# An encoder trunk whose engine order is planned: new prices in the planner, a later request for the norm rows, another packing

## The chip, the cores and the metric

The kernel runs on one core of a Trainium2 chip. The metric is the device time of one execution in microseconds; the median of three executions stands for it. One more execution was profiled, and everything that is read below from a trace comes from that one.

## The reference

Two layers work on x of 512 positions by 1024 features, all in float32. One layer computes

```
h = RMSNorm(x);  z = h @ w_in                 # 1024 x 4352: q,k,v of branch A, q,k,v of branch B, gates ga, gb
A = windowed attention (8 heads, 2 kv heads, RoPE, sink, window 128)
B = 2-D neighbourhood attention (8 heads, 8x16 window on an 8x64 grid, relative bias)
x = x + (sigmoid(ga) * (A @ w_proj_a) + sigmoid(gb) * (B @ w_proj_b)) @ w_out
x = x + (silu(h' @ w_gate) * (h' @ w_up)) @ w_down     # h' = RMSNorm(x), hidden width 2816
```

In both attention branches q and k are normalised per head before the scores, and the softmax runs over at most 384 (A) or 256 (B) keys of a query.

## The kernel before

x is held transposed, as eight tiles `xT[k]` of 128 features by 512 positions. Every large product is made of float32r products: each operand is split into a high part (a cast on ScalarE) and a low part (the subtraction on VectorE, or an accumulating DMA), and a block of 128 by 128 by 512 takes three matmuls: high by high, high by low, low by high. This is a *unit* of the main stream (`UNIT` in the code). `token_matmul` and `pair_matmul` yield after each unit.

A layer's main stream is `layer(l)`: q of branch A (32 units, `token_matmul`), k and v of branch A (16 units, `pair_matmul` with `kv_evac`), q and k of branch B, v of branch B, again q and k of branch B (32 units each), the gates (128 units), the two output projections of the branches (64), `w_out` (64), the first hidden block of the feed-forward part (16 for gate, 16 for up), and then five larger hidden blocks. For these a seven-product scheme of 2 by 2 quadrants is used: `m_step` does one of the seven products (24 matmuls of 256 columns) in the order 1, 5, 6, 2, 7, 3, 4. It needs a split of a combination of weights (class `Quad`) and a split of a combination of x's blocks (`chain_x`, which fills `xs[m]`). Behind product 1 a ScalarE copy (`seed`) puts its sum into a second PSUM bank, and product 6 adds to that bank.

Beside the main stream run *chains*, generators for the norm, the head norms, RoPE, each head of attention, the splits of x's blocks. A chain yields a `Need`: which tiles must be ready for which engine, which PSUM banks must be free. `Norm.chain` sums the squares on TensorE, computes the inverse root (`rsqrt`: some fourteen small VectorE operations, each on the result of the one before) and then turns the factor into rows with four transposes, which makes `nrm.rows`.

The order of each engine's instructions is fixed before the kernel runs, in a first pass without a chip: each call of an engine (class `Engine`) advances a clock of that engine by a price (`cost`), and writes down when the result is ready. A reader on another engine, or on the same one, sees it ready later by a hop (`HOPS`). A chain goes on when its `Need` is met at the main stream's clock: for TensorE the tiles must be ready `MARGIN` (0.3) ahead; for the others the engine's clock may lead TensorE's by at most a backlog (`BACKLOG` 1.0 us, `XLOG` 6.0 us). Where the main stream yields a name, as `f"rows{nrm.i}"`, `force` issues chains, with ever more slack, until that name is done. The second pass issues the same order, and every engine works its queue strictly in that order.

The first pass also notes from when to when each buffer is used. `Layout.pack` places the buffers in two arenas of fixed size: it tries five orders of placing, takes the first that fits, and then `spread` moves buffers so that one that takes the place of another comes long after it. `spread` returns a histogram of the time between the two, the shortest (negative) bin first.

Line 305 in all rows is the one line through which all instructions are issued, so the rows are told apart by tile: `mm` and `at` are PSUM banks (main products; attention, transposes and some quadrants), `arena` is any buffer, `sm` and `hf` are small tiles of factors, `rstd` the norm factor, `negm` the negative maximum of a score row, `gb` a column of gains.

Of the kernel before, what the change touches and what calls it, by code (L numbers as in the profile page):

```python
# [25 lines left out]
KD = D // P  # L26
FFN = 2816
QUADS = (FFN - 256) // 512
ARENAS = {F32: 20480, F32R: 32128}
# [4 lines left out]
XLOG = 6.0  # L34
# [61 lines left out]
class Layout:  # L96
# [40 lines left out]
    def pack(self):  # L137


        starts = [0] * len(self.sizes)  # L140
        self.slack = {}
        for kind in ARENAS:
            live = [i for i, k in enumerate(self.kinds) if k == kind and self.uses[i] is not None]
            u = np.array([self.uses[i] for i in live])
            size = np.array([self.sizes[i] for i in live])
            span = u[:, 1] - u[:, 0]
            orders = [
                np.lexsort((-span, -size)),
                np.argsort(-span * size, kind="stable"),
                np.argsort(-span, kind="stable"),  # L150
                np.lexsort((-span * size, -size > -1000)),
                np.lexsort((u[:, 0], -size)),
            ]
            at = next((f for o in orders if (f := self.packed(u, size, o, ARENAS[kind])) is not None), None)
            if at is None:
                raise RuntimeError(f"no room in the arena for {kind}")
            self.slack[kind] = self.spread(u, size, at, ARENAS[kind])
            for i, x in zip(live, at):
                starts[i] = int(x)
        self.starts = starts  # L160
        self.dry, self.count = False, 0
# [48 lines left out]
def trunk(ctx: ExitStack, tc: tile.TileContext, a: dict, out: bass.AP, lay: Layout):  # L210
# [20 lines left out]
    def buf(shape, dtype=F32):  # L231

        n = int(np.prod(shape))
        x = lay.place(n, dtype)
        t = arenas[dtype][:, x : x + n]
        if len(shape) == 2:
            t = t.rearrange("p (a b) -> p a b", b=shape[1])
        elif len(shape) == 3:
            t = t.rearrange("p (a b c) -> p a b c", b=shape[1], c=shape[2])
        return t  # L240
# [7 lines left out]
    def mm_bank():  # L248
        return pm.tile([P, S], F32, tag="mm", name=nm("mm"))
# [9 lines left out]

    clock = {"pe": 0.0, "dve": 0.0, "act": 0.0, "pool": 0.0, "dma": 0.0}  # L260
    ready = {}
    HOPS = {("pe", "dve"): 0.2, ("pe", "act"): 0.2, ("dve", "pe"): 0.26, ("act", "pe"): 0.3, ("dve", "dve"): 0.06}

    def at_(tensor, key):

        t, by = ready.get(tensor, (0.0, key))
        return t + HOPS.get((by, key), 0.0 if by == key else 0.15)


    def cost(eng, name, o, aps):  # L270
        n = max(x.free_size() for x in aps) / 1000.0
        in_psum = any(x.space == PS for x in aps[1:])
        if eng == "pe":
            cols = aps[2].free_size()
            if name == "transpose":
                return 0.1
            if aps[1].dtype == F32:
                return max(4 * cols, 256) / 2400.0 + 0.002
            return 0.12 if cols == 256 else (cols if cols >= 256 else 4 * cols) / 2255.0
        if eng == "act":  # L280
            return n * 0.833 + (0.06 if in_psum else 0.1) + 0.093 * sum(x.free_size() == 1 for x in aps[2:])
        if eng == "dve":
            fast = name in ("tensor_copy", "tensor_scalar") and not in_psum
            per = 0.52 if fast else 6.4 if name == "reciprocal" else 1.04
            return n * per + (0.13 if name == "scalar_tensor_tensor" and not in_psum else 0.075)
        return n * 2.2 + 0.1

    steps = [0]
# [143 lines left out]
    def tick(dt):  # L432
        pos[0] += dt
        while due and due[0][0] <= pos[0]:
            due.pop(0)[2]()
# [126 lines left out]
    def w_take():  # L562

        i = used[0]
        used[0] += 1
        w_load(i)
        w_low(i)
        return [(highs[i][:, k], lows[i][:, k]) for k in range(plan[i][0])]
# [108 lines left out]
    def mm(ps, l_, r_, start, stop):  # L677
        T.matmul(ps, l_, r_, start=start, stop=stop, skip_group_check=True)
# [58 lines left out]
    def gain(norm, k):  # L737
        c = 16 * (norm % 2) + 8 * (norm // 2) + k
        return vecT[:, c : c + 1]
# [117 lines left out]
    def pair_matmul(parts, xh, xl, evac):  # L857

        ps = [mm_bank(), mm_bank()]
        for k0 in range(0, parts, 4):  # L860
            n = min(4, parts - k0)
            wk = w_take()
            for j in range(2):
                c = slice(P * j, P * j + P)
                for k in range(n):
                    kk = k0 + k
                    hi, lo = wk[k]
                    mm(ps[j], hi[:, c], xh[kk], kk == 0, False)
                    mm(ps[j], hi[:, c], xl[kk], False, False)
                    mm(ps[j], lo[:, c], xh[kk], False, kk == parts - 1)  # L870
                    tick(UNIT)
                    if kk == parts - 1:
                        evac(j, ps[j])
                    yield UNIT
# [314 lines left out]
    def layer(l):  # L1189
        nrm = norms[2 * l]  # L1190
# [173 lines left out]

        yield from token_matmul(nrm, copy_to(qraw), (lambda *x: start(nrm, *x)) if l == 0 else None)
        done.add(f"q{l}")
        yield f"rows{nrm.i}"

        def kv_evac(j, ps):
            t = act()  # L1370
# [3 lines left out]
                V.tensor_tensor(by_columns(t), held(ps), held(nrm.rows), ALU.mult)  # L1374
            kv.append(t)

        yield from pair_matmul(KD, nrm.xh, nrm.xl, kv_evac)
        done.add(f"kv{l}")
        yield from token_matmul(nrm, copy_to(qk[0]))
        done.add(f"qk{l}0")  # L1380
# [58 lines left out]
        nrm = norms[2 * l + 1] = Norm(2 * l + 1)  # L1439
# [34 lines left out]
        def chain_x():  # L1474
            yield Need(keys=[f"rows{nrm.i}"])
            xn = [buf([4, S]) for _ in range(2)]
            (b11, b12), (b21, b22) = ((t[:, :, :256], t[:, :, 256:]) for t in xn)

            def normal(h):
                for i in range(4):  # L1480
                    yield Need(backlog=XLOG)
                    V.scalar_tensor_tensor(
                        xn[h][:, i], xT[4 * h + i], gain(nrm.i, 4 * h + i), nrm.rows, ALU.mult, ALU.mult
                    )

            def high(m, src):
                yield Need("act", [src], backlog=XLOG)
                h = buf([4, 256], F32R)
                A.copy(h, src)
                xs[m] = src, h  # L1490

            def low(m):
                src, h = xs[m]
                yield Need("dve", [h], backlog=XLOG)
                lo = buf([4, 256], F32R)
                V.tensor_tensor(lo, src, h.bitcast(F32), ALU.subtract)
                xs[m] = h, lo
                done.add(f"x{l}{m}")

            n1, n2 = buf([4, 256]), buf([4, 256])  # L1500
            yield from normal(0)
            yield from high(1, b11)
            V.tensor_tensor(n1, b11, b12, ALU.subtract)
            yield from low(1)
            yield from high(5, n1)
            yield from normal(1)
            V.scalar_tensor_tensor(n2, n1, -1.0, b22, ALU.mult, ALU.subtract)
            yield from high(6, n2)
            yield from low(5)
            yield from low(6)  # L1510
            yield from high(2, b21)
            yield from low(2)
            V.tensor_tensor(b12, b22, b12, ALU.subtract)
            yield from high(7, b12)
            yield from low(7)
            yield from high(3, b22)
            yield from low(3)
            V.scalar_tensor_tensor(n1, n2, -1.0, b21, ALU.mult, ALU.subtract)
            yield from high(4, n1)
            yield from low(4)  # L1520
# [4 lines left out]
        u = []  # L1525
# [122 lines left out]
        for i, step in enumerate(steps_[:-KD]):  # L1648
            if step[0] == "m":
                _, q, w, m = step  # L1650
# [4 lines left out]
            else:  # L1655
                _, f0, n, c = step
# [5 lines left out]
                o = mm_bank()  # L1662
# [4 lines left out]
        _, f0, n, _ = steps_[-1]  # L1667
# [12 lines left out]
    def main():  # L1680
        norms[0] = Norm(0)
        for l in range(DEPTH):
            yield from layer(l)
# [30 lines left out]
```

## Time and profile before

| what | us |
|---|---|
| median of three runs | 1396.6 |
| lowest and highest run | 1396.34 and 1397.06 |
| profiled execution, its own time | 1397.06 |
| its span in the trace | 1395.3 |
| TensorE busy in the span | 1374.3 |
| VectorE, ScalarE, GpSimd busy | 916.6, 699.5, 317.5 |

The span is the stretch from the first to the last instruction of the program; the profiled execution's own time is 1.8 us longer. A row of a timeline gives the start, the time to the end of the last of its instructions, and in brackets the idle time of that engine before it with the engine and tile that ended it. The attention part of the two layers lies at about 36 to 256 us and 720 to 939 us; the feed-forward quadrants begin at 379.6 and 1062.5 us.

### The profile page before, as it was taken

How to read it: one execution, taken by the hardware profiler on the slowest of the kernel's cores; microseconds unless marked ns; L12 is line 12 of the kernel's file. 1: busy time of each engine (PE TensorE's matmuls, PEld its weight loads, DVE VectorE, ACT ScalarE, POOL GpSimd, SP SyncE). 2: the span in 40 equal slices, each digit the busy share in tenths (PEclk: the TensorE clock that was granted, in tenths of full speed). 3: DMA queues.
4: the chain of work that ended last, by engine and by line, in shares of the span. 5: the costliest groups of instructions: out<-in, count | busy, mean ns of one | idle time of the engine just before them, and what ended most of it. 6: DMA issues, size and time to landing. Idle time of an engine off the chain costs nothing.

```text
span 1395.3 us, 20880 instructions
## 1 busy us (share of the span) xinstructions
PE 1374.3 (98%) x8042; PEld 1210.4 (87%) x8042; DVE 916.6 (66%) x1718; ACT 699.5 (50%) x1155; POOL 317.5 (23%) x326
## 2 busy tenths in 40 slices
PE   7999999999999999999999999999999999999998
PEld 5788888888899999999987888888888999999996
DVE  5876888455877566575648768773568747575653
ACT  6477667444644343343545776664356334333441
POOL 4443222310121020101353422223012110111110
PEclk9999999999999999999999999999999999999999
DMA  8888888974676475735799878889558583754645
GB/s 210 170 156 144 153 148 151 179 172 152 114 173 146 112 180 122 181 78 120 151 190 191 141 139 153 154 146 214 139 136 144 140 202 87 169 121 121 143 86 119
DMA packets 197331, 207.45 MB, mean 149 GB/s; under 512 B 25568, under 2 KB 167056, under 8 KB 197232
## 3 DMA queue, kind: packets, MB, share of 16 engines
q0 software_dynamic: 134976, 141.54, 54.7%
q1 hardware_dynamic: 61904, 64.04, 16.0%
q8 instruction: 63, 1.03, 0.3%
q10 hardware_dynamic: 352, 0.54, 0.1%
q14 instruction: 36, 0.29, 0.1%
HBM read 193.51 MB, written 2.10 MB: 140 GB/s over the span
## 4 chain that ended last, share of the span: by engine, by line
PE 82%; DVE 10%; DMA 3%; ACT 2%; issue 2%; POOL 0%; SPq 0%; DVEq 0%; ACTq 0%; POOLq 0%
PE mm L305 64%; PE at L305 18%; DVE arena L305 7%; DVE sm L305 3%; ACT arena L305 2%; DMA arena<-in_rel_bias_b 1%; DMA arena<-in_w_in 1%; DMA arena<-arena 1%; DMA cst<-in_consts 0%; DVE hf L305 0%; SPq L305 0%; POOL posi L305 0%; ACT L305 0%; POOL vec L305 0%; ACT mm L305 0%
## 5 line engine op out<-in xcount | busy, mean ns | idle before, releaser
L305 PE MATMUL mm<-arena 128*128 128x512 f32 (+1 forms) x5568 | 1114.3, 356 | 4.6 <-ACT arena L305 1.9
L305 PEld LDWEIGHTS mm<-arena 128*128 128x128 f32 x5568 | 905.0, 190 | 139.2 <-DVE arena L305 4.2
L305 ACT CAST arena<-arena 128x1024 fp32r<-128x1024 f32 (+2 forms) x278 | 235.5, 869 | 210.3 <-DVE arena L305 204.0
L305 DVE TENSOR_TENSOR arena<-arena,arena 128x1024 fp32r<-128x1024 f32 (+2 forms) x268 | 262.4, 994 | 60.7 <-ACT arena L305 60.1
L305 ACT ACTIVATE arena<-arena 128x1024 fp32r<-128x1024 f32 (+3 forms) x252 | 206.3, 842 | 155.3 <-DMA arena<-in_w_down 80.2
L305 PE MATMUL at<-arena 128*128 128x256 f32 (+1 forms) x1952 | 279.7, 288 | 1.3 <-DVE arena L305 1.3
L305 PEld LDWEIGHTS at<-arena 128*128 128x128 f32 x1952 | 258.6, 191 | 15.0 <-DVE arena L305 1.6
L305 DVE TENSOR_TENSOR arena<-arena,mm 128x512 f32<-128x512 f32 x144 | 98.8, 686 | 232.0 <-PE mm L305 232.0
L305 POOL DMA_DIRECT2D arena<-in_w_in x163 | 162.3, 1408 | 324.1 <-ACT arena L305 315.6
L305 POOL DMA_DIRECT2D arena<-in_w_down x96 | 98.1, 1229 | 500.9 <-ACT arena L305 389.2
L305 DVE TENSOR_TENSOR arena<-arena 128x1024 f32<-128x1024 f32 (+4 forms) x196 | 158.4, 823 | 2.4
L305 DVE TENSOR_TENSOR arena<-at,arena 128x512 fp32r<-128x512 f32 (+4 forms) x158 | 103.9, 659 | 26.1 <-ACT arena L305 21.0
L305 ACT CAST arena<-at 128x512 fp32r<-128x512 f32 (+2 forms) x116 | 64.1, 554 | 75.9 <-PE at L305 74.5
L305 PE MATMUL at<-cst,arena 128*128 128x128 f32 x472 | 74.9, 277 | 5.0 <-DVE arena L305 3.8
L305 ACT ACTIVATE arena<-arena,negm 128x256 f32<-128x256 f32 (+1 forms) x128 | 68.3, 534 | 18.0 <-DVE negm L305 16.4
L305 DVE TENSOR_TENSOR arena<-mm,arena 128x512 f32<-128x512 f32 x72 | 49.2, 686 | 39.2 <-PE mm L305 39.1
L305 PEld LDWEIGHTS at<-cst,arena 128*128 128x128 f32 x472 | 57.6, 141 | 19.2 <-DVE arena L305 4.5
L305 ACT COPY arena<-at 128x512 f32<-128x512 f32 (+1 forms) x68 | 39.5, 581 | 66.2 <-PE at L305 65.8
L305 DVE CUSTOM_DVE_ANT_0 arena<-at,cst,nsnk 128x256 f32<-128x256 f32 (+1 forms) x64 | 34.3, 547 | 29.9 <-PE at L305 29.6
L305 ACT ACTIVATE arena<-arena,vecT 128x512 fp32r<-128x512 f32 x24 | 17.4, 726 | 53.7 <-DVE arena L305 53.3
L305 DVE CUSTOM_DVE_ANT_0 arena<-at,arena 128x256 f32<-128x256 f32 x64 | 26.4, 420 | 17.6 <-PE at L305 17.2
L305 DVE TENSOR_SCALAR arena<-arena,sm 128x256 f32<-128x256 f32 (+1 forms) x104 | 37.2, 414 | 1.1
(68 smaller groups left out, 392.9 us busy)
## 6 DMA issues: line engine op xcount, KB each, us to landing
arena<-in_w_in POOLq DMA_DIRECT2D x99, 512.0 KB, 7.2
arena<-in_w_down POOLq DMA_DIRECT2D x80, 512.0 KB, 6.7
arena<-in_w_gate SPq DMA_DIRECT2D x20, 1024.0 KB
arena<-in_w_up SPq DMA_DIRECT2D x20, 1024.0 KB
arena<-in_w_in POOLq DMA_DIRECT2D x64, 256.0 KB, 6.6
arena<-in_w_proj_a POOLq DMA_DIRECT2D x16, 512.0 KB, 7.3
arena<-in_w_proj_b POOLq DMA_DIRECT2D x16, 512.0 KB, 7.3
arena<-in_w_out SPq DMA_DIRECT2D x16, 512.0 KB
```

Of the source, the lines that this page charges most:

```text
L305: f(*args, **kw)
```

## The change

Five prices of the plan change: a VectorE operation that reads the result of a VectorE operation sees it 0.115 us after its end (0.06 before); ScalarE after ScalarE 0.12 (none before); `scalar_tensor_tensor` that reads PSUM costs 0.15 more; `scalar_tensor_tensor` in SBUF 0.055 less; `tensor_scalar` with a column of factors 0.055 more. The main stream asks for the rows of the attention norm after nine of the sixteen units of k and v instead of ahead of them. The casts of x's blocks (`high` in `chain_x`) wait until ScalarE's clock is at most 1 us ahead of TensorE's, instead of 6 us. `pack` places the buffers in all of the five orders that fit, and takes the one whose histogram is the smallest, bin by bin from the shortest.

```diff
-            at = next((f for o in orders if (f := self.packed(u, size, o, ARENAS[kind])) is not None), None)
-            if at is None:
+            fits = [f for o in orders if (f := self.packed(u, size, o, ARENAS[kind])) is not None]
+            if not fits:
                 raise RuntimeError(f"no room in the arena for {kind}")
-            self.slack[kind] = self.spread(u, size, at, ARENAS[kind])
+            self.slack[kind], _, at = min((self.spread(u, size, f, ARENAS[kind]), i, f) for i, f in enumerate(fits))
...
-    HOPS = {("pe", "dve"): 0.2, ("pe", "act"): 0.2, ("dve", "pe"): 0.26, ("act", "pe"): 0.3, ("dve", "dve"): 0.06}
+    HOPS = {("pe", "dve"): 0.2, ("pe", "act"): 0.2, ("dve", "pe"): 0.26, ("act", "pe"): 0.3, ("dve", "dve"): 0.115, ("act", "act"): 0.12}
...
             per = 0.52 if fast else 6.4 if name == "reciprocal" else 1.04
-            return n * per + (0.13 if name == "scalar_tensor_tensor" and not in_psum else 0.075)
+            wait = 0.0
+            if name == "scalar_tensor_tensor" and in_psum:
+                wait = 0.15
+            elif name == "tensor_scalar" and any(x.free_size() == 1 for x in aps[2:]):
+                wait = 0.055
+            return n * per + 0.075 + wait
...
         done.add(f"q{l}")
-        yield f"rows{nrm.i}"
...
-        yield from pair_matmul(KD, nrm.xh, nrm.xl, kv_evac)
+        for i, unit in enumerate(pair_matmul(KD, nrm.xh, nrm.xl, kv_evac)):
+            yield unit
+            if i == KD:
+                yield f"rows{nrm.i}"
...
             def high(m, src):
-                yield Need("act", [src], backlog=XLOG)
+                yield Need("act", [src])
```

## Rows read from the trace of the kernel before

**Rows 1.** The page, part 1: busy time of each engine and share of the span.
```profile
PE 1374.3 (98%) x8042; PEld 1210.4 (87%) x8042; DVE 916.6 (66%) x1718; ACT 699.5 (50%) x1155; POOL 317.5 (23%) x326
```
**Rows 2.** Stretches: length; busy (count) of PE, PEld, DVE, ACT, POOL; clock; DMA; GB/s.
```profile
36.00:256.00 220.00, 215.97 (x1149) 182.28 (x1148) 171.26 (x500) 144.50 (x313) 71.64 (x72) 1.00 0.84 153
...
362.00:390.00 28.00, 27.42 (x161) 24.14 (x160) 26.70 (x42) 20.02 (x24) 9.45 (x9) 1.00 0.78 143
...
720.00:939.00 219.00, 216.57 (x1148) 183.30 (x1148) 165.67 (x476) 143.44 (x312) 71.73 (x72) 1.00 0.86 156
```
**Rows 3.** TensorE's waits: total us, times, longest us.
```profile
PE at L305 <- DVE arena L305: 5.1, 11, 1.5
...
PE at L305 <- DVE rstd L305: 1.7, 1, 1.7
PE mm L305 <- DVE arena L305: 1.6, 4, 0.6
PE mm L305 <- ACT mm L305: 1.2, 2, 0.6
PE at L305 <- DVE negm L305: 0.8, 2, 0.4
```
**Rows 4.** TensorE's groups from 255.5 to 379.2 us: count, busy us, mean ns.
```profile
L305 PE MATMUL mm<-arena 128*128 128x512 f32 x541 | 123.4, 389 | 0.0
```
**Rows 5.** TensorE's timeline, layer 0, from 36 to 71 us.
```profile
38.51 1.65 PE L305 MATMUL mm<-arena 128*128 128x512 f32 x6
41.82 0.62 PE L305 MATMUL at<-cst,rstd 128*128 128x128 f32 x4 [1.66 <-DVE rstd L305]
42.20 11.85 PE L305 MATMUL mm<-arena 128*128 128x512 f32 x51
...
67.48 0.30 PE L305 MATMUL at<-cst,arena 128*128 128x128 f32 x1 [0.88 <-DVE arena L305]
```
**Rows 6.** TensorE's timeline, layer 1, from 705 to 752 us.
```profile
711.64 0.60 PE L305 MATMUL at<-cst,rstd 128*128 128x128 f32 x4
...
750.73 0.30 PE L305 MATMUL at<-cst,arena 128*128 128x128 f32 x1 [0.75 <-DVE arena L305]
```
**Rows 7.** VectorE's timeline: steps that depend on each other.
```profile
41.12 0.16 DVE L305 TENSOR_TENSOR sm<-sm 128x4 f32<-128x4 f32 x1
41.32 0.16 DVE L305 SCALAR_TENSOR_TENSOR sm<-sm,sm 128x4 f32<-128x4 f32 x1
41.51 0.16 DVE L305 SCALAR_TENSOR_TENSOR rstd<-sm,sm 128x4 f32<-128x4 f32 x1
```
**Rows 8.** VectorE's timeline: four steps that do not depend on each other.
```profile
367.43 2.74 DVE L305 SCALAR_TENSOR_TENSOR arena<-arena,vecT 128x512 f32<-128x512 f32 x4
```
**Rows 9.** VectorE's groups over the whole span: count, busy us, mean ns.
```profile
L305 DVE SCALAR_TENSOR_TENSOR arena<-at,gb,arena 64x512 fp32r<-64x512 f32 x16 | 12.0, 750 | 2.6 <-ACT arena L305 2.2
L305 DVE SCALAR_TENSOR_TENSOR arena<-arena,vecT 128x512 f32<-128x512 f32 x16 | 10.9, 747 | 0.1
```
**Rows 10.** TensorE's timeline: shorter waits within attention, layer 0.
```profile
102.76 0.44 PE L305 MATMUL at<-arena 128*128 128x384 f32 x1 [0.27 <-DVE arena L305]
...
182.69 0.47 PE L305 MATMUL at<-arena 128*128 128x256 f32 x2 [0.37 <-DVE arena L305]
...
201.25 0.55 PE L305 MATMUL at<-cst,arena 128*128 128x128 f32 x3 [0.19 <-DVE arena L305]
...
223.65 0.66 PE L305 MATMUL at<-cst,arena 128*128 128x128 f32 x4 [0.38 <-DVE negm L305]
```
**Rows 11.** TensorE's timeline: the first quadrant products and the last transposes.
```profile
379.59 5.91 PE L305 MATMUL at<-arena 128*128 128x256 f32 x48
386.08 3.14 PE L305 MATMUL mm<-arena 128*128 128x256 f32 x24 [0.58 <-ACT mm L305]
...
1390.35 0.63 PE L305 MATMUL at<-cst,arena 128*128 128x128 f32 x4 [1.47 <-DVE arena L305]
```
**Rows 12.** ScalarE's and VectorE's timelines at the first quadrant products.
```profile
383.31 1.03 ACT L305 CAST arena<-arena 128x1024 fp32r<-128x1024 f32 x1
...
385.46 0.57 ACT L305 COPY mm<-at 128x512 f32<-128x512 f32 x1
...
380.93 3.48 DVE L305 TENSOR_TENSOR arena<-arena,arena 128x1024 fp32r<-128x1024 f32 x3
...
387.02 1.23 DVE L305 TENSOR_TENSOR arena<-arena,arena 128x1024 fp32r<-128x1024 f32 x1 [0.27 <-ACT arena L305]
```

## The prediction

> **What bounds the kernel now.** I read the busy shares first: TensorE is busy for 1374.3 of 1395.3 us, VectorE for 916.6 [rows 1]. So the end is set by the length of TensorE's stream, and a change that adds or removes no matmul can only act through the 21.0 us in which TensorE stands. Next the stretches [rows 2]: 4.0 us of this lies in layer 0's attention (220.00 less 215.97), 2.4 us in layer 1's (219.00 less 216.57) and 0.6 us where the feed-forward part begins. In attention VectorE is busy for 171.3 of 220 us, and at the start of the feed-forward part for 26.7 of 28. Then TensorE's waits by releaser [rows 3]: nearly all of them end with a VectorE operation. The transposes wait 5.1 us for VectorE in eleven places, of which one, 1.47 us at 1390.35, is the tail of the kernel and out of the change's reach [rows 11].
>
> The idle time in a row understates a wait. A 512-column matmul lasts 389 ns in the record, but 541 of them take 123.4 us [rows 4], one each 0.227 us (with some transposes in between). A wait behind such a matmul is therefore about 0.16 us longer than the idle time printed; I add this to each below.
>
> **The rows asked for later.** In layer 0 TensorE finishes q at about 40.2 us and stands 1.66 us for `rstd` [rows 5], 1.82 us with the hidden part. Behind it wait the 51 matmuls of k and v and more, all of which need only the split of x. With the change nine units of three matmuls, 27 x 0.227 = 6.1 us, come first, which is more than 1.82. So the wait goes: -1.8 us. Without that cover it costs 1.8 again. What is late next: the row copy is needed by the second bank of k and v, seven units or 4.8 us after the ninth unit at the latest, and a VectorE copy fits into that. VectorE's own chain is not moved: it still starts from the same sums. In layer 1 the same four transposes run at 711.64 without any wait [rows 6], so nothing is won there. No DMA is issued in the moved step, and the two queues that fetch weights follow a count of units which is not touched.
>
> **The longer steps.** Dependent VectorE steps start 0.19 to 0.20 us apart at 0.16 us each [rows 7], which is 0.03 us after the end of the one before. Independent ones start (2.74 - 0.747) / 3 = 0.664 us apart at 0.747 us each [rows 8, 9], which is 0.08 us ahead of it. The difference is 0.11 us: the new hop (0.115) fits this, the old one (0.06) was 0.055 short. So the plan believed chains of VectorE to be ready earlier than they are, and TensorE, which works in order, met them too soon. The Trainium skill says the opposite of the rows here (VectorE: DVE Perf Modes, "The DRAIN you can't avoid"): the next operation waits for the pipe to empty anyway, and a semaphore between two of them costs nothing extra. By that sentence a dependent step is no later than an independent one, the right hop is 0, and the longer hop would win none of what follows. The trace does not agree, by the 0.11 us above.
>
> What hangs on it, wait by wait. (a) The transposes of k behind RoPE wait 0.88 us at 67.48 and 0.75 us at 750.73 [rows 5, 6], 1.95 us with the hidden parts. The chain ahead of them has six steps of `rsqrt` and three of the head norm whose price rises, and two in each of four RoPE blocks: 17 x 0.055 = 0.94 us later in the plan, close to each wait. I take 1.6 us of 1.95. (b) Eight shorter waits on `arena`, four of each layer with 182.69 and 201.25 among them [rows 10]: 5.1 less the tail's 1.47 and less 1.63 is 2.0 us of idle time, 3.3 us with eight hidden parts. Two of them (182.69 and its twin) are behind `scalar_tensor_tensor` from PSUM with `gb`, 750 ns each [rows 9], whose price rises by 0.15 twice in a row; three are behind the scaling of the probabilities by a column, up by 0.055 in up to four steps; for the rest (102.76 and its twin, a subtraction from PSUM) no price changes. I take 2.1 of 3.3 us. (c) Two waits for `negm`, 0.8 us idle [rows 3, 10], 1.1 us in all: the price of that operation is untouched, so I take 0.2.
>
> Against this stands that every later choice of the plan falls anew, and new waits of the kind in (b) and (c) will come up. Their bounds are nothing and what is there now, 4.4 us; I take +1.0, near the lower bound, since the prices now err less. Work that the plan puts later is covered as long as the main stream has gates left: after the last head product at 255 us there are about 541 / 3 = 180 units, of which 160 are projections, `w_out` and the first feed-forward block, so some 20 units of gates, 20 x 0.68 = 13.8 us, are spare. Four waits in the start-up (1.6 us [rows 3]) are behind VectorE too; the tables' chain beside them gets longer steps, so it may move by a few tenths either way: taken as 0, bounds -1.0 and +1.0.
>
> **The casts of x.** At 386.08 product 6 waits 0.58 us (0.74 with the hidden part) for the `seed` copy [rows 11], which stood in ScalarE's queue behind a cast of 1.03 us and others and ran at 385.46 [rows 12]; the same happens in layer 1 (two waits, 1.2 us idle in all [rows 3]). With casts held back the copy can stand further forward: at best -1.5 us for both layers. But the chain of x's blocks is one sequence: a held cast also holds the VectorE work behind it, and VectorE has only 1.3 us of 28 free there [rows 2]. The low parts at 380.93 leave little: the first of the three is done by about 382.1, product 5 begins at about 382.5 (half of the 5.91 us that start at 379.59). At worst the lead that is given up, 6 - 1 = 5 us, less those 0.4 us is lost in each layer: +9.2 us. The row nearest to it is the wait itself, so I take -0.4.
>
> **The packing** removes no instruction. TensorE's waits show none that ends with an old reader of a buffer in the arena, so I take 0; bounds -0.5 and +1.0, as a poor place would cost a wait like those of (b).
>
> **Sum.** -1.8 (rows) - 1.6 - 2.1 - 0.2 (longer steps) + 1.0 (new waits) - 0.4 (casts) = -5.1 us. From the profiled execution's 1397.06 this gives 1392.0; that execution is 0.5 us above the median of 1396.6, so I forecast 1391.5.
>
> **Rivals.** *The waits move and do not vanish.* The plan errs by more than its prices (a maximum's accumulator step, a subtraction from PSUM, TensorE's own short switches are priced as before), and asked at other times it misses as often. Only the rows and the casts remain: 1.8 + 0.4 = 2.2 us, time 1394.4. For it: (c) and half of (b) are not touched by any price. Against it: the two longest waits lie behind exactly the chains that were priced short. The skill's sentence above would lead to this case too. *The held casts make VectorE late (slower than before).* At each start of the feed-forward part VectorE idles until ScalarE's clock in the plan is within 1 us; x's fifth and sixth splits then come late and TensorE stands. With the full 4.6 us in each layer and 4.7 us won elsewhere: 1396.6 + 9.2 - 4.7 = 1401.1. It makes the change slower than before from 2.4 us lost in each layer on. For it: VectorE is full in that stretch. Against it: ScalarE waits there for VectorE, not the reverse, so its clock rarely runs ahead. *Nothing late at all*: every wait named goes and none comes: 1.8 + 1.95 + 3.3 + 1.1 + 1.5 = 9.6 us, 1387.0.
>
> **Chances.** Forecast, with its own range 1388.5 to 1394: 0.64. Waits that move: 0.21. Held casts: 0.11. Nothing late: 0.04. A difference under 0.2%, 2.8 us, cannot be told from none. Faster: nearly all of 0.64, all of 0.04 and few of 0.21, 0.68. Same: most of 0.21 and little of the forecast's upper end, 0.20. Slower: the held casts and a bad new plan, 0.12. The range of 8 in 10 goes from 1387.5 to 1398.5: it takes in the moved waits and leaves out most of the held casts.
>
> **What would show it.** After: the wait for `rstd` in layer 0 gone and matmuls of k and v ahead of its transposes; the two k transposes with under 0.3 us of idle time; TensorE's waits on VectorE in attention down from about 4.4 (with `negm`) to some 2 us; `seed` earlier and no new wait before products 5, 6 or 2. The prediction is wrong if the idle time of TensorE in the two attention stretches stays above 5 us together, or if product 5 or 2 waits for a split of x.

## The result and the profile after

The changed kernel takes 1389.1 us (six runs, 1388.87 to 1389.48) against 1396.7: a ratio of 0.9944, 95% interval 0.9934 to 0.9954, or 7.6 us less. The forecast was 1391.5. The profiled execution took 1389.13 us with a span of 1387.4, so the spans differ by 7.9 us.

The page's busy shares and the stretches of [rows 1, 2], after (the columns are those of these rows; line 310 is to the changed kernel what line 305 is to the kernel before):

```profile
PE 1370.7 (99%) x8042; PEld 1211.2 (87%) x8042; DVE 910.7 (66%) x1702; ACT 708.3 (51%) x1171; POOL 317.3 (23%) x326
```
```profile
36.00:256.00 220.00, 219.51 (x1171) 187.66 (x1172) 167.87 (x490) 147.85 (x319) 74.33 (x74) 1.00 0.86 157
362.00:390.00 28.00, 26.34 (x176) 24.23 (x175) 25.06 (x30) 18.82 (x24) 8.18 (x8) 1.00 0.78 144
720.00:939.00 219.00, 218.56 (x1164) 186.65 (x1163) 164.14 (x469) 147.54 (x317) 70.83 (x71) 1.00 0.86 158
```

TensorE's idle time in the two attention stretches fell from 4.0 and 2.4 us to 0.5 and 0.4; where the feed-forward part begins it rose from 0.6 to 1.7. TensorE's waits by releaser, to be read against [rows 3]:

```profile
PE at L310 <- DMA vec<-in_ffn_norm_g: 4.1, 1, 4.1
PE mm L310 <- DVE mm L310: 3.4, 2, 1.7
PE at L310 <- issue: 1.4, 1, 1.4
PE mm L310 <- ACT arena L310: 1.3, 1, 1.3
PE mm L310 <- DVE arena L310: 1.1, 3, 0.7
PE at L310 <- DVE negm L310: 0.4, 2, 0.2
PE at L310 <- DVE arena L310: 0.3, 1, 0.3
```

The 5.1 us of `at <- DVE arena` are 0.3, but 1.4 of what is missing has only changed its name: the wait of the last transposes, 1.47 us before [rows 11], still stands at 1382.46 with 1.42 us and is the row of `issue` here. So 3.6 us became 0.3. `rstd` is gone. Behind the wait for the first transfer, which was there before, a new row stands on top: two waits of 1.7 us of a product for a VectorE operation that writes a bank. TensorE's timeline from 30 to 75 us and from 366 to 390 us, against [rows 5, 11]:

```profile
36.16 1.02 PE L310 MATMUL at<-ones,arena 128*128 128x1 f32 x8 [0.31 <-DVE arena L310]
37.04 4.37 PE L310 MATMUL mm<-arena 128*128 128x512 f32 x18
41.25 0.60 PE L310 MATMUL at<-cst,rstd 128*128 128x128 f32 x4
...
64.45 0.60 PE L310 MATMUL at<-cst,arena 128*128 128x128 f32 x4
...
372.79 6.04 PE L310 MATMUL at<-arena 128*128 128x256 f32 x48
378.67 3.04 PE L310 MATMUL mm<-arena 128*128 128x256 f32 x24
381.55 3.04 PE L310 MATMUL at<-arena 128*128 128x256 f32 x24
386.24 3.95 PE L310 MATMUL mm<-arena 128*128 128x256 f32 x31 [1.66 <-DVE mm L310]
```

Eighteen matmuls run between the sums and the transposes of `rstd` where six ran before, and nothing waits. The transposes of k at 64.45 do not wait either. Product 6 starts at 378.67 with no wait for `seed`; product 7 at 386.24 waits.

To see where time went in each kernel below, I cut every trace at the same points of the work: the first `at<-ones` matmul of each of the four norms, and the first matmul of the first and of the eleventh quadrant product. The stretches between are in us, from the profiled execution of each. That can lie up to 3.2 us from the median of its kernel; the clock falls in some executions and not in others (experiments 2 and 3, and the last section):

| kernel | start-up | attention to w_out, layer 0 | ten products, layer 0 | attention to w_out, layer 1 | ten products, layer 1 |
|---|---|---|---|---|---|
| before | 37.7 | 322.8 | 36.5 | 336.8 | 36.5 |
| changed | 36.2 | 317.5 | 37.7 | 333.3 | 37.8 |
| rows alone | 37.1 | 319.2 | 36.5 | 336.8 | 36.5 |
| prices alone | 36.1 | 318.6 | 39.3 | 333.1 | 37.8 |
| casts alone | 37.1 | 322.8 | 41.0 | 337.1 | 39.6 |
| packing alone | 37.0 | 322.8 | 36.5 | 337.5 | 36.5 |
| changed, casts undone | 35.8 | 317.5 | 40.9 | 333.1 | 41.2 |
| changed, rows undone | 38.0 | 319.3 | 39.4 | 333.3 | 39.3 |
| changed, hops undone | 39.0 | 321.1 | 41.0 | 338.1 | 39.0 |
| changed, costs undone | 37.9 | 317.9 | 43.4 | 333.5 | 41.3 |
| changed, ScalarE's hop undone | 36.9 | 317.5 | 37.3 | 333.1 | 37.3 |
| old prices in the feed-forward part | 36.1 | 317.9 | 37.6 | 333.1 | 36.6 |
| changed, two casts early | 36.4 | 317.5 | 37.7 | 333.3 | 37.7 |
| changed, w_down's copy later | 36.4 | 317.5 | 36.1 | 333.1 | 36.1 |

What is left out (19.1 us from the second norm's sums to the first product, and the rest of the feed-forward part) is the same within 0.6 us in all but one, where it is said. The changed kernel's 7.9 us are -1.5 - 5.3 + 1.2 - 3.5 + 1.2.

### The profile page after: what moved, and what is told of

It reads as the page before. It is cut to its first block, busy times and chain, and to the rows that moved or that the text cites. A ratio compares the mean times of both kernels' runs of the same rounds, so it can differ in the third digit from the quotient of the medians.

```text
span 1387.4 us, 20895 instructions
## 1 busy us (share of the span) xinstructions
PE 1370.7 (99%) x8042; PEld 1211.2 (87%) x8042; DVE 910.7 (66%) x1702; ACT 708.3 (51%) x1171; POOL 317.3 (23%) x326
## 4 chain that ended last, share of the span: by engine, by line
PE 90%; DVE 2%; issue 2%; ACT 2%; DMA 2%; POOL 0%; POOLq 0%; ACTq 0%
PE mm L310 71%; PE at L310 19%; ACT arena L310 2%; DVE arena L310 2%; DMA arena<-in_w_down 1%; DMA arena<-in_w_in 1%; DVE sm L310 0%; DMA cst<-in_consts 0%; POOL arena L310 0%; ACT L310 0%; POOL posi L310 0%; POOL vec L310 0%; DVE mm L310 0%; ACT trig L310 0%; ACT sm L310 0%
## 5 line engine op out<-in xcount | busy, mean ns | idle before, releaser
L310 PE MATMUL at<-arena 128*128 128x256 f32 (+1 forms) x1952 | 282.8, 289 | 0.4 <-DVE negm L310 0.4
L310 POOL DMA_DIRECT2D arena<-in_w_up x8 | 8.2, 1030 | 126.7 <-PE mm L310 79.1
```

What stands on the lines that cost most here:

```text
L310: f(*args, **kw)
```

## The experiments

**1. The rows alone.** The kernel before with this edit:

```diff
-        yield f"rows{nrm.i}"
...
+        for i, unit in enumerate(pair_matmul(KD, nrm.xh, nrm.xl, kv_evac)):
+            yield unit
+            if i == KD:
+                yield f"rows{nrm.i}"
```

> The kernel before with the later request for the rows alone. Theory 1 (each wait of TensorE that goes is won): the wait for rstd in layer 0 (1.66 us idle, 1.82 us with the hidden part) goes and nothing takes its place: 1396.7 - 1.8 = 1394.9 us. Rival (VectorE sets the pace from there on): TensorE comes 1.8 us earlier to the transposes of k behind RoPE, their wait of 0.88 us grows to about 2.7 us, and the time stays at 1396.7 us.

Measured: 1393.1 us, ratio 0.9975 (0.9965 to 0.9984), 3.5 us less. The wait of the k transposes did not grow, so VectorE does not set the pace:

```profile
41.46 0.60 PE L305 MATMUL at<-cst,rstd 128*128 128x128 f32 x4
...
64.67 0.33 PE L305 MATMUL at<-cst,arena 128*128 128x128 f32 x1 [0.72 <-DVE arena L305]
```

More than 1.8 us went, because layer 0's attention was planned anew: the waits at 102.76, 182.69 and 201.25 of [rows 10] are not there, and one new wait of 0.34 us is. With 0.16 us added to each, the printed waits make 2.8 of the 3.6 us by which the stretch is shorter. On the final plan the edit is worth what was forecast: layer 0's stretch is 319.3 us with it undone and 317.5 with it (experiment 6).

**2. The prices alone.**

```diff
-    HOPS = {("pe", "dve"): 0.2, ("pe", "act"): 0.2, ("dve", "pe"): 0.26, ("act", "pe"): 0.3, ("dve", "dve"): 0.06}
+    HOPS = {("pe", "dve"): 0.2, ("pe", "act"): 0.2, ("dve", "pe"): 0.26, ("act", "pe"): 0.3, ("dve", "dve"): 0.115, ("act", "act"): 0.12}
...
-            return n * per + (0.13 if name == "scalar_tensor_tensor" and not in_psum else 0.075)
...
+            return n * per + 0.075 + wait
```

> The kernel before with the five new prices of the plan alone. Theory 1: the waits behind VectorE in attention were there because dependent steps were priced short; the two k transposes lose their waits, the shorter waits go too, and the changed kernel's gain of 7.6 us is nearly all here: with 1.8 us for the rows taken off and 2.2 us added back that the changed kernel loses where the feed-forward part begins, 1396.7 - 8.0 = 1388.7 us. Rival (a new plan merely draws other waits): 1396 to 1398 us.

Measured: 1392.0 us (1390.17 to 1393.43), ratio 0.9965 (0.9953 to 0.9978). Attention gains 4.2 and 3.7 us, the start-up 1.6. The feed-forward part loses: product 6 now waits 1.82 us for `seed` in both layers, and in layer 0 the clock fell after it. TensorE's timeline, then three stretches (columns as in [rows 2]; the granted clock is the third figure from the right):

```profile
373.84 5.91 PE L310 MATMUL at<-arena 128*128 128x256 f32 x48
381.57 4.27 PE L310 MATMUL mm<-arena 128*128 128x256 f32 x24 [1.82 <-ACT mm L310]
```
```profile
380.00:383.10 3.10, 1.53 (x13) 1.53 (x13) 3.09 (x3) 2.51 (x4) 1.37 (x3) 1.00 1.13 142
383.10:386.50 3.40, 3.40 (x19) 3.40 (x18) 3.37 (x6) 2.09 (x3) 1.20 (x2) 0.50 1.05 316
386.50:396.00 9.50, 9.50 (x75) 9.27 (x75) 3.18 (x5) 3.29 (x5) 1.91 (x2) 1.00 0.69 126
```

So attention and the start-up won 9.5 us and the quadrants gave back 4.0, a loss that I had put down to the casts.

**3. The casts alone.**

```diff
-                yield Need("act", [src], backlog=XLOG)
+                yield Need("act", [src])
```

> The kernel before with x's casts held back alone. Theory 1 (the held casts fall behind ScalarE's steps that wait for a weight transfer, VectorE then stands, and a product waits for the addition that fills its bank): TensorE's wait in the first quadrant products grows from 0.58 to about 1.7 us idle in both layers, 1396.7 + 2.2 = 1398.9 us. Rival (the forecast: the seed copy moves forward): 1396.7 - 0.4 = 1396.3 us or less, down to 1395.2 us.

Measured: 1404.4 us, ratio 1.0061 (1.0047 to 1.0075), 7.7 us more: worse than either theory. VectorE stands 1.45 us for a cast, the split for product 5 comes late, and the addition before product 7 later still. VectorE's timeline, then TensorE's in layer 0 and in layer 1:

```profile
374.50 1.23 DVE L305 TENSOR_TENSOR arena<-arena,arena 128x1024 fp32r<-128x1024 f32 x1 [1.45 <-ACT arena L305]
```
```profile
383.15 3.02 PE L305 MATMUL at<-arena 128*128 128x256 f32 x23 [1.01 <-DVE arena L305]
386.01 3.04 PE L305 MATMUL mm<-arena 128*128 128x256 f32 x24
388.89 3.04 PE L305 MATMUL at<-arena 128*128 128x256 f32 x24
394.30 7.93 PE L305 MATMUL mm<-arena 128*128 128x256 f32 x50 [2.37 <-DVE mm L305]
...
1070.91 3.02 PE L305 MATMUL at<-arena 128*128 128x256 f32 x23 [1.01 <-DVE arena L305]
...
1082.05 10.12 PE L305 MATMUL mm<-arena 128*128 128x256 f32 x77 [2.36 <-DVE mm L305]
```

The waits of the two layers are equal, yet the ten products took 41.0 us in layer 0 and 39.6 in layer 1. In layer 0 the granted clock fell from 2.4 to 1.2 GHz behind the wait, for 3.4 us; in layer 1 it did not:

```profile
395.30:398.70 3.40, 3.40 (x18) 3.40 (x17) 1.23 (x1) 1.56 (x2) 1.91 (x2) 0.51 0.61 226
...
1082.00:1085.40 3.40, 3.35 (x28) 3.38 (x29) 0.00 (x0) 1.57 (x2) 0.66 (x1) 1.00 1.00 352
```

One such fall costs about 1.5 us, the difference of 41.0 and 39.6 before rounding. The same difference stands between the layers with the prices alone (39.3 and 37.8).

**4. The packing alone.**

```diff
-            at = next((f for o in orders if (f := self.packed(u, size, o, ARENAS[kind])) is not None), None)
+            fits = [f for o in orders if (f := self.packed(u, size, o, ARENAS[kind])) is not None]
...
-            self.slack[kind] = self.spread(u, size, at, ARENAS[kind])
+            self.slack[kind], _, at = min((self.spread(u, size, f, ARENAS[kind]), i, f) for i, f in enumerate(fits))
```

> The kernel before with the packing that compares all orders alone; each engine's order is that of the kernel before, only addresses differ. Theory 1 (no wait of TensorE ended with an old reader of a buffer): 1396.7 us, within 0.5 us. Rival (reuse of buffers was behind some of the waits for VectorE): the waits in attention shrink without any other order, 1 to 3 us less.

Measured: 1397.7 us (1397.12 to 1399.58), ratio 1.0009 (1.0000 to 1.0018). The waits of TensorE for buffers from VectorE did not shrink (5.8 us in ten places, 5.1 in eleven before); one of 0.92 us stands in layer 1 at 766.42, where none was printed before, and that stretch is 337.5 us. The interval leaves anything from nothing to a loss of 0.2%: what the packing does is not settled.

**5. The changed kernel with the casts undone** (the edit of experiment 3, reversed).

> The changed kernel with x's casts issued up to 6 us ahead again. Held back, they cost 7.7 us alone on the kernel before, yet the kernel with the new prices alone also stands 1.82 us for the seed copy in each layer. Theory 1 (under the new prices the two ways cost about the same: 1.82 us before product 6 in place of 1.66 us before product 7): 1389.1 + 0.3 = 1389.4 us. Rival (the held casts are a loss whatever the prices): the start of the feed-forward part returns to the 0.58 us of the kernel before, 1389.1 - 2.2 = 1386.9 us, or lower still.

Measured: 1397.5 us (1395.69 to 1399.83), ratio to the kernel before 1.0009 (1.0000 to 1.0017). Both theories fell: with the other parts in place, undoing the casts costs 8.4 us. `seed` is late by 1.82 us, as with the prices alone, and a second wait has come, for a transfer of w_down (TensorE's timeline):

```profile
380.08 3.13 PE L310 MATMUL mm<-arena 128*128 128x256 f32 x24 [1.82 <-ACT mm L310]
...
394.03 2.13 PE L310 MATMUL mm<-arena 128*128 128x512 f32 x12 [1.72 <-DMA arena<-in_w_down]
```

**6 to 8. The changed kernel with one other part undone**: the rows (the edit of experiment 1, reversed), the two hops, the costs.

```diff
-    HOPS = {("pe", "dve"): 0.2, ("pe", "act"): 0.2, ("dve", "pe"): 0.26, ("act", "pe"): 0.3, ("dve", "dve"): 0.115, ("act", "act"): 0.12}
+    HOPS = {("pe", "dve"): 0.2, ("pe", "act"): 0.2, ("dve", "pe"): 0.26, ("act", "pe"): 0.3, ("dve", "dve"): 0.06}
...
-            return n * per + 0.075 + wait
+            return n * per + (0.13 if name == "scalar_tensor_tensor" and not in_psum else 0.075)
```

> The changed kernel with the rows asked for ahead of k and v again. Theory 1: the wait for rstd comes back, 1.2 to 1.8 us with nothing else changed: 1390.5 us. Rival (the later request drew a better plan for all of layer 0's attention, as it seems to have done alone on the kernel before, where it won 3.5 us): 1392.6 us.

> The changed kernel with the old hops (0.06 from VectorE to VectorE, none from ScalarE to ScalarE) and the new costs. Theory 1 (the hop is what made VectorE's chains look ready too early): the k transposes wait about 1 us again in each layer and some shorter waits return, 1389.1 + 4 = 1393 us; the old cost of scalar_tensor_tensor made up for part of the short hop, so it may be worse than the kernel before in the root's chain. Rival (the two raised costs did it): 1389 to 1390 us.

> The changed kernel with the old costs of scalar_tensor_tensor and tensor_scalar and the new hops. Theory 1 (the hop does most): the k transposes stay without a wait, the products behind gb's splits (0.37 and 0.40 us before) and the transposes behind the scaled probabilities wait again, 1389.1 + 1.5 = 1390.6 us. Rival (the costs did it): 1393 us.

Measured: 1393.5, 1404.1 and 1399.1 us; ratios to the kernel before 0.9981 (0.9972 to 0.9989), 1.0052 (1.0040 to 1.0065), 1.0017 (1.0007 to 1.0026). None of the times forecast above was met. The whole times mislead, since the quadrants come out differently in each (39 to 43 us) and the start-up's clock fell in these three traces too. Attention answers the question: without the hops it takes 3.5 and 4.8 us more, without the costs 0.3 and 0.2. Without the hops the wait of the k transposes is back:

```profile
66.55 0.49 PE L310 MATMUL at<-cst,arena 128*128 128x128 f32 x3
67.80 0.30 PE L310 MATMUL at<-cst,arena 128*128 128x128 f32 x1 [0.76 <-DVE arena L310]
```

**9. ScalarE's hop to itself undone**, to tell the two hops apart.

```diff
-    HOPS = {("pe", "dve"): 0.2, ("pe", "act"): 0.2, ("dve", "pe"): 0.26, ("act", "pe"): 0.3, ("dve", "dve"): 0.115, ("act", "act"): 0.12}
+    HOPS = {("pe", "dve"): 0.2, ("pe", "act"): 0.2, ("dve", "pe"): 0.26, ("act", "pe"): 0.3, ("dve", "dve"): 0.115}
```

> The changed kernel with ScalarE's hop to itself taken out again; VectorE's longer hop and the new costs stay. Without both hops the attention stretches (from the first sums of the norm to the next ones) took 321.1 and 338.1 us, with both 317.5 and 333.3 us. Theory (VectorE's hop is the cause): 317.5 and 333.3 us again, each within 0.6 us. Rival (ScalarE's hop is part of it): 1 us or more lost in one of them. The whole time is not forecast from this, since the quadrants are drawn anew: 1386 to 1396 us.

Measured: 317.5 and 333.1 us, 1389.0 us in all. So attention's gain does not need ScalarE's hop, and without both hops it is gone. VectorE's hop as the only new price was not run. What ScalarE's hop wins is in the start-up, 36.9 us here against 36.2.

**10. Old prices and early casts in the feed-forward part only.** A flag is set in `layer(l)`, cleared at the start of the feed-forward part, and asked in `at_` and `cost`:

```diff
+        if by == key and not long[0]:
+            return t + (0.06 if key == "dve" else 0.0)
...
+            if not long[0]:
+                wait = 0.055 if name == "scalar_tensor_tensor" and not in_psum else 0.0
...
-                yield Need("act", [src])
+                yield Need("act", [src], backlog=XLOG)
```

> The changed kernel with the old prices, and the casts of x up to 6 us ahead, for the feed-forward part of each layer; the new prices hold for the attention part alone, the rows are asked for later and the packing is the new one. Theory (the gain is all in attention and the start-up, and the feed-forward part loses whenever its plan is drawn by the new prices): the ten quadrant products take 36.5 us in each layer again in place of 37.7, attention keeps its 5.2 and 3.5 us: 1389.1 - 2.4 = 1386.7 us. Rival (the order of the kernel before in the quadrants was a lucky draw that any other plan of attention ahead of it spoils too): 1389 us or more, with a wait of 1 to 2 us in the quadrants.

Measured: 1391.0 us (1389.51 to 1391.99), ratio 0.9956 (0.9944 to 0.9969). Layer 1's ten products are back at 36.6 us, layer 0's are not (37.6), and `seed` waits 0.59 us as before; but waits for w_down came, 1.7 us in four, and the rest of the feed-forward part took 1.3 us more in each layer. The time is the rival's. That the new prices put `seed` late was seen in experiment 2; here the old prices and the early casts come back together, so this run does not tell the two apart, and the old order in a new place is not simply good either.

**11. Two casts early.** Of x's seven casts the second and seventh with a backlog of 6 us again.

```diff
-            def high(m, src):
-                yield Need("act", [src])
+            def high(m, src, backlog=BACKLOG):
+                yield Need("act", [src], backlog=backlog)
...
-            yield from high(2, b21)
+            yield from high(2, b21, XLOG)
...
-            yield from high(7, b12)
+            yield from high(7, b12, XLOG)
```

> The changed kernel with only the second and the seventh cast of x's blocks issued up to 6 us ahead, the others held back. Theory (those two fall behind the copy for w_down that waits for its transfer): they stand ahead of it, VectorE does not stand, the wait before product 7 goes or shrinks to 0.5 us: 1389.1 - 2.3 = 1386.8 us. Rival (each cast that is issued ahead pushes the seed copy back): the seed copy is late by 0.6 to 1.8 us before product 6, 1388.5 to 1391 us.

Measured: 1389.0 us. The backlog of these two never decides: each engine works the order of the changed kernel, and product 7 waits 1.64 and 1.67 us as there. So the theory was not put to the test; the run says only that the changed kernel's time repeats within 0.2 us.

**12. The copies for w_down later.** In the changed kernel ScalarE stands for a transfer with casts behind it, VectorE stands for the casts, and the addition before product 7 (it reads the bank that product 7 writes) is late. ScalarE's timeline, then VectorE's:

```profile
377.52 0.57 ACT L310 COPY mm<-at 128x512 f32<-128x512 f32 x1
379.91 0.63 ACT L310 ACTIVATE arena<-arena 128x512 fp32r<-128x512 f32 x1 [1.81 <-DMA arena<-in_w_down]
380.45 0.57 ACT L310 COPY arena<-at 128x512 f32<-128x512 f32 x1
380.91 3.03 ACT L310 CAST arena<-arena 128x1024 fp32r<-128x1024 f32 x4
```
```profile
381.99 2.36 DVE L310 TENSOR_TENSOR arena<-arena,arena 128x1024 fp32r<-128x1024 f32 x2 [1.63 <-ACT arena L310]
384.27 1.22 DVE L310 SCALAR_TENSOR_TENSOR arena<-arena 128x1024 f32<-128x1024 f32 x1
385.40 0.69 DVE L310 TENSOR_TENSOR mm<-mm,arena 128x512 f32<-128x512 f32 x1
```

The edit moves the copies for the first four slabs of w_down in each layer:

```diff
-                    slab(n, 256, [...], 0, 3.0, 2.0)
+                    slab(n, 256, [...], 0, 3.0, 5.0 if f0 == 0 else 2.0)
```

> The changed kernel with one thing moved: for the first four slabs of w_down the copy on ScalarE ahead of the low part's transfer is issued 3 units of time later. Theory (in the changed kernel that copy stands 1.81 us on ScalarE for a transfer, two casts stand behind it, VectorE stands 1.63 us for them, and product 7 waits 1.66 us because the addition that reads its bank comes late): the wait before product 7 falls to 0.3 us or less in both layers, 1389.1 - 2.8 = 1386.3 us. Rival (VectorE's own queue is too full, whatever ScalarE does): the wait stays above 1 us and the time at 1389 us; or the low part comes too late for its product, and a wait for w_down of 1 to 2 us takes the place.

Measured: 1385.8 us (1385.62 to 1385.99), ratio to the kernel before 0.9920 (0.9906 to 0.9933): 3.3 us less than the changed kernel, as the chain of waits says, and the best version here. Its timelines of ScalarE, VectorE and TensorE:

```profile
379.50 2.01 ACT L310 CAST arena<-arena 128x1024 fp32r<-128x1024 f32 x2
381.40 0.64 ACT L310 ACTIVATE arena<-arena 128x512 fp32r<-128x512 f32 x1
```
```profile
380.59 2.36 DVE L310 TENSOR_TENSOR arena<-arena,arena 128x1024 fp32r<-128x1024 f32 x2
...
384.00 0.69 DVE L310 TENSOR_TENSOR mm<-mm,arena 128x512 f32<-128x512 f32 x1
```
```profile
381.70 3.04 PE L310 MATMUL at<-arena 128*128 128x256 f32 x24
384.84 5.38 PE L310 MATMUL mm<-arena 128*128 128x256 f32 x43
```

The casts stand ahead of the copy, none of the three engines stands for another in these rows, and product 7 starts 3.14 us behind product 2 with no idle time printed.

## Why the prediction was right, and where it was not

*The rows* (-1.8): right. On the final plan layer 0's stretch changes by 319.3 - 317.5 = 1.8 us, and layer 1's by nothing. No wait for the row copy is printed. The cover is smaller than was reckoned: not nine units of k and v run ahead of the transposes but four, the twelve matmuls that eighteen exceed six by, so the chain went on before the main stream asked for it. Twelve matmuls, 2.7 us, are still more than 1.82.

*The longer steps* (-1.6, -2.1, -0.2, and +1.0 for new waits, -2.9 in all): the mechanism is right and the size is low. Attention's stretches lost 8.8 us, 1.8 of which are the rows; 7.0 us is more than the 6.35 us that I had found as named waits. Two terms were mis-sized. One is the share taken of the named waits, 1.6 + 2.1 + 0.2 = 3.9 us of 6.35: the k transposes lost their waits whole, and so did the eight shorter ones (three in layer 0 and five in layer 1, not four of each), with 102.76 and its twin among them, for which no price changed; the waits for `negm` came down from 0.8 to 0.4 us of idle time though their price did not change. That makes about 5.6 us. The other is "Against this stands that every later choice of the plan falls anew ...; I take +1.0": no new wait of note came in attention, where only the two for `negm`, 0.22 us each, are left. The remaining 1.4 us stand in no printed wait. A wait below 0.16 us shows no idle time, by the prediction's 389 and 227 ns, so they may lie there; that was not shown. That VectorE's hop is the cause, and not the costs, was shown by experiments 7 to 9, with the other parts in place. (Without the hops the loss is 8.3 us, more than 7.0; the new costs, which are lower for `scalar_tensor_tensor` in SBUF, stood in that run beside the old hops.) By the sentence of the Trainium skill that was weighed ahead (VectorE: DVE Perf Modes, "The DRAIN you can't avoid") the longer hop would have won nothing; with the hop back at 0.06 the waits return, so the runs do not agree with it. The same section of the Trainium skill does not say the opposite of the rows in all, as the prediction has it: it adds that a next operation which is not held starts earlier. The independent steps, which start 0.08 us ahead of the end of the one before [rows 8, 9], agree with that.

*The start-up* (0, bounds -1.0 and +1.0): -1.5 us in these traces, and the tenths that were left open have a cause. Two waits of the kernel before stand in all six kernels in which ScalarE has no hop to itself, and in none of the eight in which it has one (kernel before, TensorE's timeline):

```profile
32.21 0.74 PE L305 MATMUL mm<-arena 128*128 128x512 f32 x2 [0.42 <-ACT arena L305]
...
33.48 0.50 PE L305 MATMUL mm<-arena 128*128 128x512 f32 x1 [0.53 <-DVE arena L305]
```

With that hop alone undone (experiment 9) they are 0.38 and 0.53 us, and the start-up takes 36.9 us in place of 36.2: ScalarE's hop wins 0.7 us. Another 0.6 us is the execution: the kernel before took 37.7 us, and with the casts or the packing alone, where TensorE works the same order, it was 37.1 and 37.0.

*The casts* (-0.4): the step failed, in sign on the kernel before and in size in the changed one. "At best -1.5 us" was reckoned as if the rest of the plan stood still. Alone the edit costs 7.7 us, by the very mechanism that stood as the slower rival: VectorE stands for a held cast, and products 5 and 7 for VectorE. Among the other parts it wins 8.4 us. There the first half of the step holds, since product 6 does not wait for `seed`, for which it waits 1.82 us with the casts undone; but the held casts also take part in the chain of experiment 12, which costs 1.66 and 1.72 us of idle time before product 7. "Nearest row" was a bad guide: the 0.74 us wait for `seed` said nothing of what the queue would hold once it was drawn anew.

*What the forecast left out*: it priced the longer steps in attention only. With the prices alone `seed` stands behind more casts (0.58 to 1.82 us of idle time), and in the changed kernel, where it does not, the ten products still took 1.2 us longer in each layer. Attention and the start-up won 8.8 + 1.5 = 10.3 us where 4.7 was forecast, and the quadrants lost 2.4 us where a gain of 0.4 was forecast: two errors of opposite sign, which leave 7.9 us against 5.1. That the forecast time came so near is in part luck.

*The spare work* (some 20 units of gates) was right to be looked at: after the last head product of layer 0 there are now 420 + 18 + 60 = 498 matmuls up to the quadrants, or 166 units, 6 of them gates, 4.1 us at 0.68 us each. Attention ends later, at 258 us in place of 255. By this estimate a second gain of this size would find little cover; it was not tried.

```profile
258.46 95.39 PE L310 MATMUL mm<-arena 128*128 128x512 f32 x420
353.69 0.95 PE L310 MATMUL at<-ones,arena 128*128 128x1 f32 x8
354.50 4.39 PE L310 MATMUL mm<-arena 128*128 128x512 f32 x18
358.72 0.60 PE L310 MATMUL at<-cst,rstd 128*128 128x128 f32 x4
359.08 13.87 PE L310 MATMUL mm<-arena 128*128 128x512 f32 x60
```

Still open: why the order with the casts undone brings w_down late, and whether the packing does anything.

## What to carry to other kernels

When a planner's prices change, read the stages apart: here attention won 8.8 us, 7.0 of them by prices of which the trace confirms the one that matters, the quadrants lost 2.4 us in the same kernel, and single parts added up to +0.5 us (-3.5 - 4.7 + 7.7 + 1.0) where together they won 7.6. In a queue that is worked in order, look for the instruction that waits for a transfer ahead of urgent work: moving four such copies in each layer won 3.3 us. Measure a dependent step's start-to-start time against an independent one's before you plan with it.

## What the runs showed of the hardware

A wait of TensorE of about 2 us can cost more than itself: behind waits of 1.82 us (prices alone) and 2.37 us (casts alone) the granted clock was 0.50 and 0.51 for 3.4 us in layer 0, 1.2 GHz in place of 2.4, and stayed at 1.00 in layer 1 behind waits of the same length. It was worth about 1.5 us each time. The layer does not decide it: with the casts undone the clock fell in layer 1 and not in layer 0, behind 1.82 us in both, and with the rows undone in both layers. In the six traces with waits of 1.80 to 2.37 us at the quadrants it fell behind nine of thirteen; behind the 1.66 and 1.72 us of the changed kernel it did not.

The times of one kernel's executions go with the clock: with the rows undone the runs at a mean granted clock of 0.999 took 1391.7 to 1393.0 us, those at 0.996 took 1395.0 to 1396.7. The clock is not the only cause of a wide spread, though: the packing alone and experiment 10 spread over about 2.5 us without a wait of that length at the quadrants.
